# A hybrid encoder on one core: layer norm in a fixed order with five first columns, four gate tiles, a finish in PSUM

## The chip, the cores and the metric

The kernel runs on one core of a Trainium2 chip. A core has TensorE (PE) for matmuls, VectorE (DVE), ScalarE (ACT) and GpSimd (POOL) for elementwise work, and SyncE (SP), whose queue issues most DMA transfers. The metric is the device time of one execution in microseconds (us). Each number is compared as the median of several runs of one kernel on one chip.

## The reference

The reference is a small encoder of two layers over one sequence of 256 tokens and 2048 channels, in float32: a Conformer convolution module, a feed-forward block, a bidirectional gated DeltaNet, a feed-forward block, and a last RMSNorm. What matters here of it:

```python
def layernorm(x, g, b, eps=LN_EPS):
    xf = x.astype(jnp.float32)
    mu = jnp.mean(xf, axis=-1, keepdims=True)
    xc = xf - mu
    var = jnp.mean(xc * xc, axis=-1, keepdims=True)
    return (xc * lax.rsqrt(var + eps) * g.astype(jnp.float32) + b.astype(jnp.float32)).astype(x.dtype)

def conformer_conv_module(h, w_pw1, b_pw1, w_dw, b_dw, ln_g, ln_b, w_pw2, b_pw2):
    """pointwise D->2D + GLU -> depthwise conv (31, centred) -> LayerNorm over channels -> swish -> pointwise D->D."""
    u = h @ w_pw1 + b_pw1
    a, gate = jnp.split(u, 2, axis=-1)
    u = a * jax.nn.sigmoid(gate)
    u = depthwise_conv_centred(u, w_dw) + b_dw
    u = jax.nn.silu(layernorm(u, ln_g, ln_b))
    return u @ w_pw2 + b_pw2
...
```

The DeltaNet has 16 key heads and 32 value heads of 128 channels. Each value head gives an output o of 256 tokens by 128 channels; it is normed, multiplied with a gate silu(z) of its own, and the 32 gated heads together are multiplied with the output weights.

## The kernel before

All activations lie with channels on the 128 partitions and the 256 tokens along the free axis, so the 2048 channels are 16 tiles of 128 by 256. Float32 accuracy is kept by halves: a weight block of 128 by 512 (`CS` = 4 blocks of 128 inputs) is cast on ACT to `hi` (L172), and DVE takes the rest as `lo` = raw - hi (L173); activations are split the same way into a tile of 512 columns, high half and low half. A product of an input block with a column of 128 outputs is then a matmul of `hi` with 512 columns (L198) and one of `lo` with 256 (L197, L200): a pair. Elsewhere three matmuls of 256 columns do the same (L202 to L204).

Weights come in raw tiles of 8 input blocks (`CK`, 512 KB), issued on SP (L159), three of them in the pool (`RAW`), a further three of a second pool while `self.more` is set. `products` works several columns side by side (three first columns of a projection, which begin as soon as the first input tiles are there), `linear` one column. A scheduler places instructions by priority; a stretch under `manual_schedule` stands on DVE and ACT in the order in which it is written.

**End of the convolution module.** For each of 16 channel tiles j, 31 taps of the depthwise convolution are shared out: `NPE[j]` go to PE as matmuls with diagonal matrices (`r`, L373, two passes each), `NPOOL[j]` to ACT and POOL (ACT scales `m`, L381, POOL adds, L382), two to ACT and DVE alone, the rest to DVE (L388, L390). The results are added to the tile `a` (L394). The sum of a tile goes to PE (`s1`), its square `lsq` (ACT, L337) too (`s2`); after the last tile the mean `dm`, its square `dq` and the variance `var` follow on DVE, a square root on ACT, a reciprocal on DVE, and then for each tile a product, a difference, a silu, a cast and a difference for the low half `y` (L424 to L433). These are the inputs of the second pointwise projection (weights `pw2`), whose three first columns wait for `var` before their weights are split.

**DeltaNet.** `dn_gate` computes the gate of a head and stores it to `z_d`. `dn_heads` works a group of four value heads: outputs `ot` are scaled by `os`, transposed on PE (L945), copied by ACT (`on`, L947), multiplied with the gate on DVE (`zr`, L949 to L950) and stored to `y_d` (L951). There is one `zr` tile. A task with nothing left to wait for is taken up again step by step between the projections' columns; `gated` counts the gates done. Afterwards the out projection (weights `wout`) loads the 32 heads from `y_d` (four `y` tiles, L525), splits them into `ys` (L234, L235), and runs its three first columns.

**Finish.** After the last feed-forward block `finish` multiplies the 16 tiles with the reciprocal `rstd` (L986), every third on POOL, and issues 16 output transfers on SP and ACT in turn (L987).

## Time and profile before

| | |
|---|---|
| runs | 2828.8, 2833.96, 2838.57 us; median 2833.96 |
| the profiled execution | 2831.13 us, of it the span 2829.3 |
| mean granted clock of TensorE | 0.992 of full speed |
| PE busy | 2754.5 us, 97% |
| weight loads of PE | 2508.4 us, 89%, beside the matmuls |
| DVE busy | 2070.5 us, 73% |
| ACT busy | 1760.6 us, 62% |
| POOL busy | 367.6 us, 13% |
| DMA | 533.91 MB, mean 189 GB/s |

PE is the busy engine, and most of its time is in matmuls that follow one another without a pause. The chain of work that ended last is PE for 81% of the span, DVE for 6%, ACT and DMA for 5% each. The stages in time: first pointwise projection with the convolution until about 258 us, the norm and second projection until 362, the first feed-forward block, the DeltaNet's projections and heads from about 1100 to 1915, the out projection from about 1880, the second feed-forward block, and the finish from about 2815.

### The profile page before, as it was taken

What the parts mean: (1) busy time and instruction counts of PE and PEld (TensorE: products, weight loads), DVE (VectorE), ACT (ScalarE), POOL (GpSimd) and SP (SyncE); (2) the same over time, 40 slices, a digit from 0 to 9 for tenths busy, and PEclk for the clock granted to TensorE, in tenths of its full rate; (3) what the DMA queues carried; (4) which work ended last, traced back from release to release, by engine and by line L of the source; (5) the groups of instructions that cost most, each with busy time, mean ns of one, the idle gap of its engine ahead of it and who ended that gap; (6) DMA issues with size and microseconds to landing.
All of it is one profiled execution on the core that took longest, in us unless ns stands there. A gap on an engine that the chain in (4) does not pass through costs nothing.

```text
span 2829.3 us, 50192 instructions
## 1 busy us (share of the span) xinstructions
PE 2754.5 (97%) x18192; PEld 2508.4 (89%) x18192; DVE 2070.5 (73%) x3895; ACT 1760.6 (62%) x3710; POOL 367.6 (13%) x427
## 2 busy tenths in 40 slices
PE   8997999999999999999999999998999999999998
PEld 7997888888888889998999999987888888888887
DVE  8999876666666667898988989756666666665555
ACT  8877555555554445767878877764455555555443
POOL 3764310000000011000000000001110000000111
PEclk9998999999999999999999999999999999999999
DMA  5443665555666665765565655575566655566664
GB/s 186 142 142 97 194 210 191 187 191 188 190 190 191 197 201 176 246 219 189 185 218 187 201 194 195 178 237 184 189 209 190 189 190 190 188 190 186 189 190 138
DMA packets 171801, 533.91 MB, mean 189 GB/s; under 512 B 19073, under 2 KB 43905, under 8 KB 171553
## 3 DMA queue, kind: packets, MB, share of 16 engines
q1 hardware_dynamic: 170256, 529.42, 58.5%
q8 instruction: 142, 2.33, 0.3%
q10 hardware_dynamic: 1296, 1.30, 0.1%
q14 instruction: 107, 0.87, 0.1%
HBM read 501.22 MB, written 29.43 MB: 188 GB/s over the span
## 4 chain that ended last, share of the span: by engine, by line
PE 81%; DVE 6%; ACT 5%; DMA 5%; issue 2%; POOL 1%; SPq 0%; DVEq 0%; POOLq 0%; ACTq 0%
PE acc L198 40%; PE acc L197 20%; PE acc L204 5%; PE acc L203 5%; PE acc L202 5%; DVE lo L173 2%; POOL a L382 1%; DMA raw<-in_win 1%; ACT hi L172 1%; PE psa L852 1%; PE psb L894 1%; DMA y_d<-zr 1%; PE acc L200 1%; PE psb L917 1%; DVE r L390 1%
## 5 line engine op out<-in xcount | busy, mean ns | idle before, releaser
L173 DVE TENSOR_TENSOR lo<-raw,hi 128x512 fp32r<-128x512 f32 x1764 | 1259.7, 719 | 648.5 <-ACT hi L172 640.4
L172 ACT CAST hi<-raw 128x512 fp32r<-128x512 f32 x1764 | 1079.5, 619 | 839.9 <-PE acc L198 660.1
L198 PE MATMUL acc<-xs,hi 128*128 128x512 f32 x2816 | 967.3, 392 | 0.0
L197 PE MATMUL acc<-xs,lo 128*128 128x256 f32 x2640 | 743.5, 282 | 0.0
L198 PEld LDWEIGHTS acc<-xs,hi 128*128 128x128 f32 x2816 | 516.8, 188 | 100.0
L202 PE MATMUL acc<-xs,hi 128*128 128x256 f32 x2064 | 587.3, 286 | 15.5 <-ACT hi L172 9.2
L204 PE MATMUL acc<-xs,lo 128*128 128x256 f32 x2064 | 586.7, 285 | 3.8 <-DVE lo L173 3.8
L203 PE MATMUL acc<-xs,hi 128*128 128x256 f32 x2064 | 585.0, 284 | 0.9 <-DVE xs L251 0.7
L197 PEld LDWEIGHTS acc<-xs,lo 128*128 128x128 f32 x2640 | 498.2, 189 | 8.3
L198 PE MATMUL acc<-hs,hi 128*128 128x512 f32 x1408 | 486.8, 391 | 0.0
L202 PEld LDWEIGHTS acc<-xs,hi 128*128 128x128 f32 x2064 | 389.8, 189 | 21.7 <-ACT hi L172 12.3
L204 PEld LDWEIGHTS acc<-xs,lo 128*128 128x128 f32 x2064 | 389.5, 189 | 10.8 <-DVE lo L173 6.3
L203 PEld LDWEIGHTS acc<-xs,hi 128*128 128x128 f32 x2064 | 390.2, 189 | 7.5 <-issue 5.2
L197 PE MATMUL acc<-hs,lo 128*128 128x256 f32 x1376 | 388.1, 282 | 0.0
L198 PEld LDWEIGHTS acc<-hs,hi 128*128 128x128 f32 x1408 | 262.3, 188 | 53.4
L197 PEld LDWEIGHTS acc<-hs,lo 128*128 128x128 f32 x1376 | 259.9, 189 | 1.6
L198 PE MATMUL acc<-ys,hi 128*128 128x512 f32 x512 | 179.9, 396 | 8.6 <-DVE ys L235 8.6
L463 POOL TENSOR_TENSOR tg<-tg,rstd 128x256 f32<-128x256 f32 x88 | 65.5, 744 | 905.4 <-ACT tg L462 905.4
L382 POOL TENSOR_TENSOR a<-a,m 128x256 f32<-128x256 f32 x170 | 148.7, 875 | 97.5 <-ACT m L381 85.6
L197 PE MATMUL acc<-ys,lo 128*128 128x256 f32 x496 | 140.8, 286 | 2.6 <-DVE lo L173 2.5
L261 POOL TENSOR_TENSOR sq<-h 128x256 f32<-128x256 f32 x59 | 54.6, 925 | 548.7 <-DVE h L474 384.3
L638 DVE SCALAR_TENSOR_TENSOR u<-t,par_sb,u 128x254 f32<-128x254 f32 (+1 forms) x256 | 121.3, 482 | 1.4 <-ACT u L634 1.1
(229 smaller groups left out, 2910.0 us busy)
## 6 DMA issues: line engine op xcount, KB each, us to landing
raw<-in_gu SPq DMA_DIRECT2D x352, 512.0 KB, 4.4
raw<-in_win SPq DMA_DIRECT2D x194, 512.0 KB, 4.1
raw<-in_dn SPq DMA_DIRECT2D x160, 512.0 KB, 3.6
raw<-in_pw SPq DMA_DIRECT2D x94, 512.0 KB, 3.8
raw<-in_wout SPq DMA_DIRECT2D x64, 512.0 KB, 3.7
a_d<-am SPq DMA_DIRECT2D x32, 512.0 KB, 4.6
ar<-a_d SPq DMA_DIRECT2D x32, 512.0 KB, 4.8
raw<-in_dn SPq DMA_DIRECT2D x32, 256.0 KB, 3.6
```

The source lines that it names most:

```text
L172: nc.scalar.copy(hi, r)
L173: nc.vector.tensor_tensor(lo, r, hi.bitcast(F32), op=ALU.subtract)
L197: nc.tensor.matmul(acc[:, S:], lo, a[:, :S], start=False, stop=False)
L198: nc.tensor.matmul(acc, hi, a, start=first, stop=last)
L200: nc.tensor.matmul(acc[:, S:], lo, a[:, :S], start=False, stop=False)
L202: nc.tensor.matmul(acc[:, :S], hi, a[:, :S], start=first, stop=False)
L203: nc.tensor.matmul(acc[:, :S], hi, a[:, S:], start=False, stop=False)
L204: nc.tensor.matmul(acc[:, :S], lo, a[:, :S], start=False, stop=last)
L261: (nc.vector if last else nc.gpsimd).tensor_tensor(sq, h, h, op=ALU.mult)
L382: nc.gpsimd.tensor_tensor(acc, acc, m, op=ALU.add)
L463: nc.gpsimd.tensor_tensor(tg, tg, rstd, op=ALU.mult)
L638: nc.vector.scalar_tensor_tensor(u[:, lo:hi], t[:, lo + s : hi + s], w(i), u[:, lo:hi], op0=ALU.mult, op1=ALU.add)
```

## The change

1. The last channel tile of the convolution gives 12 taps to PE and 6 to POOL, 9 and 5 before; DVE gathers its partial sums in a tile `part` before it touches the tile. The table load for the square root moves behind the last tile's scalings.
2. Five raw tiles of `pw2` are issued, and their high halves cast on ACT, before the sums end. After the last sum PE gets 26 matmuls into a tile `idle` that nobody reads (`FILL`). From `dm` to the last low half the order on DVE and ACT is written by hand, `dq` goes to ACT, and the projection starts with five columns.
3. There are four `zr` tiles in a pool of their own. The four gates of a group are loaded ahead of its transposes. The last four heads' products stay in their tiles, and the out projection splits them from there.
4. In the finish the reciprocal is written to PSUM (`own`); DVE multiplies with it there, ACT makes a copy for POOL, which takes every fourth tile.
5. At the start `Square` of the first tile is written ahead of its scaling.

```diff
-NPE = [5] * 12 + [6, 6, 6, 9]
-NPOOL = [11] * 12 + [11, 11, 11, 5]
+NPE = [5] * 12 + [6, 6, 6, 12]
+NPOOL = [11] * 12 + [11, 11, 11, 6]
...
-XB = 6
+XB = 7
+FIRSTS = 5
+PRE = 5
+FILL = 26
...
                     if own:
-                        r.append(own)
-                    for o in r:
-                        nc.vector.tensor_tensor(acc, acc, o, op=ALU.add)
+                        self.more, self.five, self.more_raw = cv, 0, 2
+                        with tc.issue_after(self.raw_dma.ins):
+                            raws = [self.raw_weights(self.pw2[c], 0, CK) for c in range(FIRSTS)]
...
+                        with tc.issue_after(scaled.ins):
+                            self.warm(AF.Sqrt, tg)
+                            for c in range(PRE):
+                                pre_hi = highs(c)
+                    if own:
+
+                        part = new("part", 1)
+                        nc.vector.tensor_copy(part, own)
+                        for o in (r[1], r[0]):
+                            nc.vector.tensor_tensor(part, o, part, op=ALU.add)
+                        t = nc.vector.tensor_tensor(acc, acc, part, op=ALU.add)
+                        weights(0, t)
+                        weights(1, t)
...
-                if j == KD - 1:
-                    self.warm(AF.Sqrt, tg)
...
+            idle = self.ps.tile([P, 512], F32, tag="lin", bufs=PSB["lin"], name=self.nm("idle"))
+            with tc.issue_after(self.summed.ins):
+                for n in range(FILL):
+                    nc.tensor.matmul(idle, pre_hi[:, :P], pre_hi, start=True, stop=True)
...
+                nc.scalar.activation(dq, sums["s1"], AF.Square, scale=1.0 / D)
+                known = nc.vector.scalar_tensor_tensor(var, sums["s2"], 1.0 / D, dq, op0=ALU.mult, op1=ALU.subtract)
+                rt = self.sp.tile([P, S], F32, tag="rstd", bufs=2, name=self.nm("rstd"))
+                nc.scalar.activation(rt, var, AF.Sqrt, scale=1.0, bias=self.c("eps5"))
+                self.warm(AF.Silu, rt)
+                weights(2)
+                nc.vector.reciprocal(lr, rt)
                 nc.vector.tensor_tensor(ml, dm, lr, op=ALU.mult)
...
+                mul(0)
+                sub(0)
+                mul(1)
+                weights(3)
+                sub(1)
+                mul(2)
+                for n in range(KD):
+                    low(n)
...
-                first = self.products(self.pw2[:3], KD, ys, wide=True, tags=("lin", "lin", "g"), pool=cv, order=order)
+            with tc.issue_after(begun.ins):
+                self.ahead, self.split_ahead = [raws], pre[:PRE]
+                first = self.products(self.pw2[:FIRSTS], KD, ys, wide=True, tags=("lin", "lin", "lin", "g", "a")[:FIRSTS], pool=cv, order=order)
...
+                    if v < NVH - 4:
+                        y = o0.tile([P, S], F32, tag="y", bufs=4, name=self.nm("y"))
+                        nc.sync.dma_start(y, self.y_d[v])
+                    else:
+                        y = self.y_last[v % 4]
...
-        "cb": (2 * S, 2), "e": (768, 2), "am": (1024, 2), "ar": (1024, 2), "zr": (S, 1), "xd": (16 * P, 2),
+        "cb": (2 * S, 2), "e": (768, 2), "am": (1024, 2), "ar": (1024, 2), "zr": (S, 4), "xd": (16 * P, 2),
...
-        yield STEP + 1
+        zs = []
         for i in range(4):
             while self.gated <= 4 * g + i:
                 yield 1
+            zs.append(self.d("zr"))
+            nc.sync.dma_start(zs[i], self.z_d[4 * g + i])
+        yield STEP + 1
+        for i in range(4):
...
-            z = self.d("zr")
-            nc.sync.dma_start(z, self.z_d[4 * g + i])
+            z = zs[i]
             nc.vector.tensor_tensor(z, on, z, op=ALU.mult)
-            nc.sync.dma_start(self.y_d[4 * g + i], z)
+            if 4 * g + i < NVH - 4:
+                nc.sync.dma_start(self.y_d[4 * g + i], z)
...
-        rstd = self.pending()
+
+        own = self.ps.tile([P, S], F32, tag="b", bufs=PSB["b"], name=self.nm("own"))
...
+        nc.scalar.copy(rstd, own)
         for k in range(KD):
             o = self.h[k]
-            (nc.gpsimd if k % 3 == 1 else nc.vector).tensor_tensor(o, o, rstd, op=ALU.mult)
+            if k % 4 == 1:
+                nc.gpsimd.tensor_tensor(o, o, rstd, op=ALU.mult)
+            else:
+                nc.vector.tensor_tensor(o, o, own, op=ALU.mult)
```

On ACT, at the end of the convolution module, the kernel before has this from the sigmoid of the last tile on (`hi` are the weights' high halves, `rstd` the square root of the norm):

```order
L355 ACTIVATE tg_3558<-tg_3558,par_sb 128x256
L278 ACT_TABLE_LOAD
L278 ACTIVATE warm_3698<-tg_3558 128x1
L378 ACTIVATE a_743_3632<-up_231,par_sb,wdw 128x256
...
L381 ACTIVATE m_3677<-up_231,wdw 128x256
L337 ACTIVATE lsq_3701<-a_743_3632 128x256
L172 CAST hi_3827<-raw_3821 128x512
...
L172 CAST hi_3871<-raw_3825 128x512
L283 ACTIVATE rstd_3712<-var_3708,cst_sb 128x256
```

And the changed kernel, in the same place:

```order
L369 ACTIVATE tg_3558<-tg_3558,par_sb 128x256
L392 ACTIVATE a_743_3632<-up_231,par_sb,wdw 128x256
...
L395 ACTIVATE m_3689<-up_231,wdw 128x256
L292 ACT_TABLE_LOAD
L292 ACTIVATE warm_3713<-tg_3558 128x1
L414 CAST hi_3715<-raw_3703 128x512
...
L181 CAST hi_3934<-raw_3705 128x512
L351 ACTIVATE lsq_3738<-a_743_3632 128x256
L466 ACTIVATE dq_3769<-s_274_1316 128x256
L469 ACTIVATE rstd_3794<-var_3770,cst_sb 128x256
```

The table load has moved behind the scalings `m` (five before, six now), and seven casts `hi` stand ahead of `lsq` where six stood behind it.

On SP, in the body of the DeltaNet, the gates of heads 8 to 11 are loaded and their products stored in the kernel before as follows (rows between left out; `zr<-z_d` is the load, `y_d<-zr` the store, `raw` weights):

```order
L951 DMA y_d7_12618<-zr_3712_17945 128x256
L949 DMA zr_3954_19195<-z_d8_12587 128x256
...
L951 DMA y_d8_12619<-zr_3954_19195 128x256
L949 DMA zr_3961_19224<-z_d9_12588 128x256
L159 DMA raw_4235_20480<-in_win 128x1024
...
L951 DMA y_d9_12620<-zr_3961_19224 128x256
L159 DMA raw_4246_20529<-in_win 128x1024
L949 DMA zr_3974_19269<-z_d10_12589 128x256
```

And in the changed kernel:

```order
L1017 DMA zr_3937_19126<-z_d8_12624 128x256
L1017 DMA zr_3938_19128<-z_d9_12625 128x256
L168 DMA raw_3927_19051<-in_win 128x1024
L1028 DMA y_d6_12654<-zr_3657_17680 128x256
L1028 DMA y_d7_12655<-zr_3658_17682 128x256
L1017 DMA zr_3939_19130<-z_d10_12626 128x256
...
L1028 DMA y_d8_12656<-zr_3937_19126 128x256
L1028 DMA y_d9_12657<-zr_3938_19128 128x256
L1017 DMA zr_4154_20068<-z_d12_12628 128x256
```

A load that stood right behind the store of the head before it now stands in pairs behind the stores of the group before, and the stores of a group come in pairs.

On DVE, in the tail of the DeltaNet, the kernel before has this from the product of head 29 on (`zr` the product, `ys` the split of a head, `lo` the weights'):

```order
L950 TENSOR_TENSOR zr_4940_23860<-on_4939_23858,zr_4940_23860 128x256
L173 TENSOR_TENSOR lo_5085_24338<-raw_5079_24327,hi_5084_24337 128x512
L173 TENSOR_TENSOR lo_5087_24366<-raw_5077_24323,hi_5086_24365 128x512
L950 TENSOR_TENSOR zr_4943_23869<-on_4942_23867,zr_4943_23869 128x256
L950 TENSOR_TENSOR zr_4946_23878<-on_4945_23876,zr_4946_23878 128x256
L235 TENSOR_TENSOR ys_5017_24057<-y_5016_24055,ys_5017_24057 128x256
```

And the changed kernel, from the product of head 30 on:

```order
L1026 TENSOR_TENSOR zr_4943_23890<-on_4950_23909,zr_4943_23890 128x256
L182 TENSOR_TENSOR lo_5085_24362<-raw_5080_24353,hi_5084_24361 128x512
L1026 TENSOR_TENSOR zr_4944_23892<-on_4952_23915,zr_4944_23892 128x256
L182 TENSOR_TENSOR lo_5087_24366<-raw_5081_24355,hi_5086_24365 128x512
L182 TENSOR_TENSOR lo_5089_24394<-raw_5079_24351,hi_5088_24393 128x512
L244 TENSOR_TENSOR ys_5023_24093<-y_5022_24091,ys_5023_24093 128x256
L244 TENSOR_TENSOR ys_5025_24098<-y_5024_24096,ys_5025_24098 128x256
L244 TENSOR_TENSOR ys_5026_24101<-zr_4941_23886,ys_5026_24101 128x256
```

The splits of heads 28 to 31 now read the tiles `zr` themselves; before, every split from head 26 on stood behind the product of head 31.

## Rows read from the trace of the kernel before

**Rows 1.** The page, busy time: engine, busy us, share of the span, instructions.

```profile
PE 2754.5 (97%) x18192; PEld 2508.4 (89%) x18192; DVE 2070.5 (73%) x3895; ACT 1760.6 (62%) x3710; POOL 367.6 (13%) x427
```

**Rows 2.** Windows: stretch, us, busy us by engine, granted clock, DMA share, GB/s.

```profile
250.00:275.00 25.00, 11.41 (x43) 9.04 (x44) 23.12 (x58) 16.08 (x35) 3.62 (x5) 0.66 0.19 64
1175.00:1878.00 703.00, 681.67 (x5716) 658.63 (x5716) 609.10 (x1337) 539.48 (x1355) 26.42 (x14) 1.00 0.61 202
...
1900.00:1926.40 26.40, 15.67 (x91) 12.98 (x89) 9.00 (x18) 11.13 (x26) 1.91 (x1) 0.85 0.48 158
1926.40:1932.40 6.00, 6.00 (x18) 5.03 (x19) 3.56 (x8) 2.37 (x5) 0.00 (x0) 0.50 0.24 71
```

**Rows 3.** Timeline of PE, 244 to 296: start, us, instruction, count, [idle before, releaser].

```profile
250.11 4.15 PE L373 MATMUL r<-up,diag 128*128 128x256 f32 x18 [0.25 <-DVE up L356]
258.03 1.22 PE L327 MATMUL s<-a,cst_sb 128*128 128x256 f32 x2 [3.77 <-DVE a L394]
...
269.82 0.80 PE L198 MATMUL acc<-y,hi 128*128 128x512 f32 x1 [9.72 <-DVE y L433]
...
273.68 0.51 PE L197 MATMUL acc<-y,lo 128*128 128x256 f32 x3
...
277.86 0.52 PE L197 MATMUL acc<-y,lo 128*128 128x256 f32 x3
```

**Rows 4.** Timeline of ACT in the same stretch.

```profile
249.55 1.28 ACT L278 ACT_TABLE_LOAD   x1
...
251.45 2.09 ACT L381 ACTIVATE m<-up,wdw 128x256 f32<-128x256 f32 x5
...
258.33 3.21 ACT L172 CAST hi<-raw 128x512 fp32r<-128x512 f32 x6
```

**Rows 5.** Timeline of DVE in the same stretch.

```profile
250.49 0.48 DVE L388 TENSOR_SCALAR own<-up,wdw 128x256 f32<-128x256 f32 x1
...
255.19 0.48 DVE L390 SCALAR_TENSOR_TENSOR own<-up,wdw,own 128x256 f32<-128x256 f32 x1
...
260.63 3.69 DVE L173 TENSOR_TENSOR lo<-raw,hi 128x512 fp32r<-128x512 f32 x6
264.24 1.76 DVE L287 RECIPROCAL ln<-rstd 128x256 f32<-128x256 f32 x1
...
266.37 0.75 DVE L424 TENSOR_TENSOR a<-a,ln 128x256 f32<-128x256 f32 x2
```

**Rows 6.** Timeline of POOL in the same stretch.

```profile
252.02 3.93 POOL L382 TENSOR_TENSOR a<-a,m 128x256 f32<-128x256 f32 x5 [4.27 <-ACT m L381]
```

**Rows 7.** Waits of SP's queue, 1090 to 1935: us in total, times, longest.

```profile
SPq L949 <- DMA y_d<-zr: 58.2, 31, 3.9
```

**Rows 8.** Waits of DVE, 1178 to 1878, same columns.

```profile
DVE zr L950 <- DMA zr<-z_d: 18.6, 10, 5.0
```

**Rows 9.** Chain of work that ended last, tail of DeltaNet: start, us, what.

```profile
1908.15 5.05 DMA y_d<-zr
...
1917.96 3.20 DMA zr<-z_d
```

**Rows 10.** Timeline of PE in the tail of DeltaNet.

```profile
1917.22 0.51 PE L197 MATMUL acc<-ys,lo 128*128 128x256 f32 x3
1926.36 1.65 PE L198 MATMUL acc<-ys,hi 128*128 128x512 f32 x3 [8.63 <-DVE ys L235]
```

**Rows 11.** Timeline of ACT in the same stretch.

```profile
1914.53 1.14 ACT L172 CAST hi<-raw 128x512 fp32r<-128x512 f32 x2 [0.97 <-DMA raw<-in_wout]
```

**Rows 12.** The page, DMA issues: count, KB each, median us to landing.

```profile
raw<-in_wout SPq DMA_DIRECT2D x64, 512.0 KB, 3.7
```

**Rows 13.** Timeline of the finish, DVE and POOL.

```profile
2819.61 6.42 DVE L986 TENSOR_TENSOR h<-h,rstd 128x256 f32<-128x256 f32 x11
2819.65 4.41 POOL L986 TENSOR_TENSOR h<-h,rstd 128x256 f32<-128x256 f32 x5 [17.49 <-DVE rstd L287]
```

**Rows 14.** Windows in the finish, columns as in rows 2.

```profile
2826.00:2828.00 2.00, 0.00 (x0) 0.00 (x0) 0.02 (x1) 0.00 (x0) 0.00 (x0) 0.50 1.09 378
```

166 lines of the change are left out of this document (96 added, 70 removed).

## Prediction

> **What bounds the kernel now.** I read the busy table first: PE works 2754.5 us of 2829.3 [rows 1], so the kernel is a string of matmuls with some 75 us of holes, and what a change can win is a hole, or a stretch at low clock. Second the windows, to find the holes: the end of the convolution module has PE busy 11.41 of 25 us at a mean granted clock of 0.66; the tail of DeltaNet, from 1900 to 1926.4, 15.67 of 26.4, and the 6 us behind it run at 0.50, which is 1.2 of 2.4 GHz; the body of DeltaNet loses 21 us spread thinly over 703 [rows 2]. Third the timelines of these places and the chain of waits, which name what each hole waits for [rows 3 to 12]. The finish behind the last matmul counts in full [rows 13, 14]. Feed-forward and the middles of the projections have no hole; the change touches them little.
>
> **The sum's base.** The profiled execution took 2831.13 us, 1.8 more than its span; the median of the runs is 2833.96. I take the gains off both and forecast on the median.
>
> **Part 1, end of the convolution module.** PE finishes its taps at 254.26, waits 3.77 us for the last tile, and after the two sums waits 9.72 us until the first y matmul at 269.82 [rows 3]. It then works cold: six pairs (a 512- and a 256-column matmul) from 269.82 to 273.68, 0.64 each, then twelve up to 277.86, 0.35 each [rows 3].
> The last tile: DVE's taps come every 0.39 us (twelve from 250.49 to 255.19) [rows 5]; four fewer save 1.56, an added copy costs 0.3. PE's 24 passes instead of 18 at 0.23 (4.15/18) [rows 3] end at 255.6, and POOL's six adds at 0.79 (3.93/5) [rows 6] at 255.9, since the table load of 1.28 that stood ahead of the last tile's scalings [rows 4] moves behind them. Both are hidden behind DVE, so the tile is ready near 256.7 instead of 258.0.
> ACT: tile, six scalings of 0.42 (2.09/5), load, then seven casts of 0.54 (3.21/6) end at 258.3 [rows 4]. The new order puts those casts ahead of the square lsq, which begins at 258.3 instead of beside the sum at 258.03 [rows 3]: what the tile won is lost again here, and s2, var and the sums behind it wait for that. In return sqrt no longer stands behind six casts, and DVE has one lo split instead of six (3.69) between var and the reciprocal. lsq 0.4, s2 0.6, var 0.4 and sqrt 0.5 put the reciprocal at 260.8 instead of 264.24 [rows 5]. Before, 5.58 us passed from there to the first y matmul; now tile 0 goes to ACT after one product and one difference, and I count 5.0, so y is ready at 265.8.
> Fillers: 26 matmuls of 512 columns stand on PE between s2 (done near 259.5) and the first y matmul, which cannot pass them. A 512-column matmul is two thirds of a pair: 0.23 warm, 0.43 cold. All warm they end at 265.6 and cost nothing, as the norm hides them. The windows show a low clock after a hole lasting 3.9 us here and 6.0 at 1926.4 [rows 2, 3]; with as much of it the fillers end between 267.4 and 268.4 and delay PE. Either way y starts warm, which saves 6 x 0.29 = 1.75.
> The Trainium skill (TensorE: Matmul & The Clock Gate, Part 1: The HAM clock gate) calls the half clock the default state, released by activity; by it the fillers pay the cold stretch themselves. The gain would be 1.4 + 1.75 = 3.2 with it, 4.0 + 1.75 = 5.8 without; the trace agrees that a hole of 9.72 us is followed by cold matmuls [rows 3] and cannot show which holds after two holes of 1.5 us.
> Five first columns instead of three: 80 pairs at 0.35 are 28 us, in which DVE has 16 x 3 norm steps at 0.33 and 16 splits at 0.6, 26 us, so PE stays the bound by a little. The second raw tiles must land beside it; I allow 0 to 1.2 us of stall. Then 11 columns remain instead of 13, the same matmuls in all. **Gain 4, between 1 and 5.8.**
>
> **Part 2, body of DeltaNet.** One zr tile makes each head's z load wait on SP until the store of the head before has landed, 58.2 us in 31 waits, and DVE stands 18.6 us in the body for z [rows 7, 8]. With four tiles and the loads ahead of the transposes, these loads wait once per pair of heads. But behind SP's wait stand weight loads that run ahead of their use, and PE's whole loss is 21 us, most of it for other reasons (chains of small products between ACT and DVE). On the other side the four loads now hold back a group's transposes until all four gates exist, and the third and fourth loads queue on SP ahead of weights. A new order of everything costs or wins some us: **gain 2, between -5 and 8.**
>
> **Part 3, tail of DeltaNet.** The last four heads go round zr by zr: product, store (5.05 for head 28), load, product, store, load (3.20 for head 30), and so on [rows 9]. PE's last matmul before the hole is at 1917.22, then it waits 8.63 us to 1926.36 for the ys splits, which stand on DVE behind zr of head 31 [rows 10]. Eighteen pairs (six heads by three columns) are left: 6.0 us cold hold 9.4 pairs, 8.6 more at 0.35 need 3.0, so they end at 1935.4.
> After: the last transposes stand in the same place of PE's queue, behind the third column of heads 20 to 23, near 1914.5; ACT's copy and DVE's product give zr of head 31 by 1916.1. Then come two splits of weights (0.6 each) and six ys splits of 0.33, to 1919.4; no store and no load is among them. The weights of these columns had landed by 1914.53 [rows 11]. PE waits at most 0.5 us, works warm, and needs 18 x 0.35 = 6.3 us from 1917.5: it ends near 1924. That is 11.4 earlier. Behind it the next column's weights must come: their buffer is free at about 1917 and a landing takes 3.7 us in the median [rows 12], so 1920.7; a cast of 0.54 and a split of 0.6 leave some 2 us. **Gain 11, between 6 and 12.**
>
> **Part 4, finish and start.** Eleven DVE products take 6.42 us, 0.58 each, beside five of POOL at 0.88 [rows 13]. After the change DVE's second operand lies in PSUM. The rows for that kind are 0.33 to 0.38 (two in 0.75, POOL idle) and 0.39 (taps on own and r, POOL adding) [rows 5, 6]. Twelve at 0.39 end at 2824.3 instead of 2826.03; POOL's copy of 0.4 and four at 0.88 end earlier, at 2823.6. The output is 2 MB, though, and the last window already moves 378 GB/s [rows 14]; begun at 2820, it cannot end before 2825.5. **Gain 1.3, between -0.6 (if DVE stays at 0.58 for twelve) and 2.** The Trainium skill (SBUF — State Buffer, SBUF: two separate sides) says that a DVE instruction with two SBUF inputs and a GpSimd one exclude each other for a whole instruction; one with a single SBUF input would be free of that. By it the gain is 1.7 less what DMA keeps; without it, -0.6. The taps, unslowed at 0.39 while POOL adds, speak for it.
> At the start Square of h0 stays ahead of xs0 as it stood: nothing.
>
> **Sum.** 4 + 2 + 11 + 1.3 = 18.3. The profiled execution becomes 2812.8, the median 2815.7; I say 2815.5. A measurement here tells 0.3%, 8.5 us, from no change.
>
> **Rivals.**
> Tail fed by weights: three raw tiles, freed only as DVE splits, land late, and PE waits for them instead of for ys. For: the last of them had landed only at 1914.53, with ACT waiting 0.97 [rows 11]. Against: SP issued them between stalled zr transfers, now gone. The gain is 4 instead of 11: 2822.5. Chance 0.12.
> Body wins more: if z's waits on DVE are what holds back the matmul feeders, half of PE's 21 us goes: 2807.5. Chance 0.12.
> Fillers do not do their work: all cold they end at 259.5 + 26 x 0.43 = 270.7, later than y's 269.82 of before; a late start by 0.9 against 1.75 saved leaves 0.9, and a stall of 1 leaves nothing: 2819.7. Chance 0.10.
> Slower: in the body PE executes in order, and a transpose that stands at its head until four z tiles exist and are gated stops all matmuls behind it. Priced at the longest wait of SP for zr, 3.9 us [rows 7], once per group of eight it costs 31 us: 2815.5 + 2 + 31 = 2848. It decides from about 2.5 us per group, where no gain is left. Against: transposes stand where they stood, and DVE's split work has slack. Chance 0.04. A milder form of it (1.5 to 3 us a group), or the bad ends of tail and body together, ends within 0.3%: 0.10.
>
> **How the numbers follow.** Forecast 0.52, between 2809 and 2822; rivals 0.12, 0.12, 0.10, 0.04, and 0.10 for a result near no change. All but the last two are faster by over 0.3%, with a few hundredths of them falling short of it: faster 0.84, same 0.12, slower 0.04. The range takes in the tail's and the filler rival together (about 2827) and the body's better end (2804): 2804 to 2828.
>
> **What would show it.** In the convolution window 250 to 275 PE busy with fillers and the first y matmul before 268.5, without the 0.64 pairs. Between 1900 and 1930 no PE wait for ys over 1 us and a granted clock of 1.00. SP's wait of zr for y_d below 30 us, PE busy in the body no less than 681 of 703. DVE's last products at 0.39 each. Wrong, if a PE wait for raw weights follows the tail, if y starts after 269, or if the body's span grows.

## The result and the profile after

The changed kernel takes 2806.19 us in the median of four runs (2802.27 to 2809.28), the kernel before 2832.56 on the same chip: a ratio of 0.9897, 95% interval 0.9882 to 0.9912. It gains 26.4 us, where 18.3 were forecast. The time lies in the range of 2804 to 2828, but 9.3 us below the predicted 2815.5. The profiled execution took 2802.27, its span 2800.5 against 2829.3.

The busy line answers to [rows 1]: PE does the same work, and what went is idle time and time at low clock.

```profile
PE 2754.0 (98%) x18224; PEld 2510.1 (90%) x18224; DVE 2065.2 (74%) x3892; ACT 1759.7 (63%) x3716; POOL 367.9 (13%) x427
```

The windows answer to [rows 2], in its columns. In the end of the convolution module PE is busy 21.91 of 25 us (11.41 before; 6.27 of the 21.91 are the 26 matmuls that nobody reads) at a clock of 1.00 (0.66); in the tail of DeltaNet, 1900 to 1926.4, 26.33 of 26.4 (15.67) at 1.00 (0.85).

```profile
250.00:275.00 25.00, 21.91 (x104) 17.56 (x105) 22.88 (x55) 19.18 (x39) 4.37 (x6) 1.00 0.17 53
1160.00:1862.00 702.00, 690.33 (x5819) 669.40 (x5818) 617.78 (x1356) 547.64 (x1378) 28.11 (x14) 1.00 0.63 208
...
1900.00:1926.40 26.40, 26.33 (x151) 23.17 (x152) 21.08 (x39) 14.78 (x29) 5.48 (x7) 1.00 0.62 199
```

Three starts cut the program at nearly the same work in these two kernels (10598 matmuls between the first two before, 10594 after): the first low-half matmul of the first feed-forward block (first `acc<-xs,lo`), the first of the out projection (first `acc<-ys,lo`) and the last of its sixteen columns. These are the groups of one line of PE with count, ns (shortest, median, longest) and first and last start, of before:

```profile
L200 PE MATMUL acc<-xs,lo x176: 281/282/469, 362.5 to 2564.8; 128*128 128x256 f32 x176
...
L200 PE MATMUL acc<-ys,lo x16: 281/282/283, 1878.8 to 2068.7; 128*128 128x256 f32 x16
```

and of after:

```profile
L209 PE MATMUL acc<-xs,lo x176: 281/281/468, 360.0 to 2537.1; 128*128 128x256 f32 x176
...
L209 PE MATMUL acc<-ys,lo x16: 280/281/282, 1862.9 to 2040.9; 128*128 128x256 f32 x16
```

From the first to the third mark, called **the stretch** below, before takes 2068.7 - 362.5 = 1706.2 us, after 1680.9. Its first piece (feed-forward and body of DeltaNet) falls from 1516.3 to 1502.9, its second (tail and out projection) from 189.9 to 178.0.

| part | forecast | measured in the two profiles |
|---|---|---|
| 1, convolution end (last matmul of the first projection to the first mark) | 4 | 114.85 to 110.9: 3.95 |
| 2, body | 2 (-5 to 8) | 13.4 |
| 3, tail | 11 (6 to 12) | 11.9 |
| 4, finish (last matmul to the end) | 1.3 | 14.62 to 13.51: 1.1 |

These sum to 30.4; the first projection itself ended 1.4 later in this execution, which leaves the 28.8 of the spans. Parts 1, 3 and 4 are near their forecasts in this profile. Part 2 is the miss, and the experiments are about it. This execution is the fastest of its four, though. A second profile of the same kernel (2807.50 us, the row "again" in the table of the experiments) gives 2.8 for part 1, 10.8 for the body, 9.4 for the tail and 1.1 for the finish.

**The end of the convolution.** Timeline of PE, columns as in [rows 3]:

```profile
251.55 5.45 PE L387 MATMUL r<-up,diag 128*128 128x256 f32 x24 [0.25 <-DVE up L370]
258.36 0.70 PE L341 MATMUL s<-a,cst_sb 128*128 128x256 f32 x2 [1.36 <-DVE a L435]
260.20 0.70 PE L341 MATMUL s<-lsq,cst_sb 128*128 128x256 f32 x2 [1.14 <-ACT lsq L351]
260.54 6.27 PE L456 MATMUL idle<-hi 128*128 128x512 f32 x26
267.00 0.50 PE L207 MATMUL acc<-y,hi 128*128 128x512 f32 x1 [0.19 <-DVE y L484]
```

The holes of 3.77 and 9.72 have become 1.36, 1.14 and 0.19, and the first y pair runs warm. The second profile has the same two holes (1.36 and 1.15), but its fillers run partly at a granted clock of 0.50, and the first y matmul, at 267.56, starts only as they end:

```profile
260.19 7.53 PE L456 MATMUL idle<-hi 128*128 128x512 f32 x26
```

ACT and DVE in the first profile, in the same stretch:

```profile
258.69 1.13 ACT L181 CAST hi<-raw 128x512 fp32r<-128x512 f32 x2
259.73 0.41 ACT L351 ACTIVATE lsq<-a 128x256 f32<-128x256 f32 x1
...
261.47 0.51 ACT L469 ACTIVATE rstd<-var,cst_sb 128x256 f32<-128x256 f32 x1 [1.06 <-DVE var L467]
```

```profile
257.88 0.42 DVE L435 TENSOR_TENSOR a<-a,part 128x256 f32<-128x256 f32 x1
...
262.01 1.76 DVE L472 RECIPROCAL ln<-rstd 128x256 f32<-128x256 f32 x1
```

Less the 1.44 us by which all this began later, the tile is ready at 256.9 (256.7 worked out), `lsq` starts at 258.3 (258.3), the reciprocal at 260.6 (260.8), y at 265.6 (265.8). Behind that the saving stops: from the first y matmul to the first mark it takes 92.97 us, 92.66 before, although y begins warm. PE waits 1.51 us there, 0.28 before.

**The tail.** Where PE waited 8.63 us [rows 10], the longest wait from 1900 to the last mark is 0.85 us, and it is for weights. DVE splits the last four heads out of the tiles `zr`, with no store and no load among them. In the second profile PE waits 3.42 us for weights earlier on: the raw tile for them took 7.31 us to land, 5.79 in the first profile. Timelines of PE and DVE, and of PE in the second profile:

```profile
1900.07 0.39 PE L206 MATMUL acc<-ys,lo 128*128 128x256 f32 x1 [0.85 <-DVE lo L182]
```

```profile
1900.54 0.75 DVE L244 TENSOR_TENSOR ys<-y,ys 128x256 fp32r<-128x256 f32 x2
1901.21 1.42 DVE L244 TENSOR_TENSOR ys<-zr,ys 128x256 fp32r<-128x256 f32 x4
```

```profile
1881.52 0.58 PE L206 MATMUL acc<-ys,lo 128*128 128x256 f32 x1 [3.42 <-DVE lo L182]
```

**The finish**, against [rows 13]: DVE 0.34 for each product (0.58 before), POOL 0.69 (0.88).

```profile
2792.32 4.07 DVE L1073 TENSOR_TENSOR h<-h,own 128x256 f32<-128x256 f32 x12 [0.44 <-ACT rstd L1067]
2792.37 2.77 POOL L1071 TENSOR_TENSOR h<-h,rstd 128x256 f32<-128x256 f32 x4 [17.90 <-ACT rstd L1067]
```

**SP's waits for the gates did not shrink.** Against the 58.2 us of [rows 7] stand 24.4 for the stores of `zr` and, new, 36.0 for the stores of the gates themselves, since the loads now stand early enough to meet them: 60.4 in all. DVE's wait for a gate in the body [rows 8] is gone. Waits of SP's queue (us in total, times, longest):

```profile
SPq L1017 <- DMA z_d<-s: 36.0, 14, 4.7
...
SPq L1017 <- DMA y_d<-zr: 24.4, 12, 3.5
```

### The profile page after: what moved, and what is told of

It is laid out like the page before. It is cut to its first block, busy times and chain, and to the rows that moved or that the text cites. A ratio compares the mean times of both kernels' runs of the same rounds, so it can differ in the third digit from the quotient of the medians.

```text
span 2800.5 us, 50212 instructions
## 1 busy us (share of the span) xinstructions
PE 2754.0 (98%) x18224; PEld 2510.1 (90%) x18224; DVE 2065.2 (74%) x3892; ACT 1759.7 (63%) x3716; POOL 367.9 (13%) x427
## 4 chain that ended last, share of the span: by engine, by line
PE 82%; ACT 6%; DVE 4%; DMA 4%; issue 2%; POOL 2%; SPq 0%; POOLq 0%; DVEq 0%; ACTq 0%
PE acc L207 39%; PE acc L206 20%; PE acc L213 5%; PE acc L212 5%; PE acc L211 5%; POOL a L396 2%; DVE lo L182 2%; PE psa L925 1%; PE psb L967 1%; ACT hi L181 1%; DMA raw<-in_win 1%; PE psb L990 1%; PE acc L209 1%; DMA raw<-in_wout 1%; PE psg L778 1%
## 5 line engine op out<-in xcount | busy, mean ns | idle before, releaser
L211 PE MATMUL acc<-xs,hi 128*128 128x256 f32 x2064 | 585.7, 285 | 13.7 <-ACT hi L181 8.9
L213 PEld LDWEIGHTS acc<-xs,lo 128*128 128x128 f32 x2064 | 389.6, 189 | 11.9 <-issue 5.7
```

What stands on the lines that cost most here:

```text
L211: nc.tensor.matmul(acc[:, :S], hi, a[:, :S], start=first, stop=False)
L213: nc.tensor.matmul(acc[:, :S], lo, a[:, :S], start=False, stop=last)
```

## Experiments

Two explanations of the body's 13.4 us stand against each other. By the first, the gate code itself (its four tiles, its early loads, the heads kept on chip) is worth more than I priced. By the second, the order: the scheduler, which places every instruction of the DeltaNet by priority, lays the whole of it out in another way as soon as anything ahead of it changes, and this layout happened to be a good one. The expectations number their theories as they stood when each was written, and call the scheduler the planner; the text between them calls the theories by what they say. Medians and ratios are against the kernel before on the same chip; "stretch" is from the profiled execution.

| kernel | median us | ratio, 95% interval | stretch |
|---|---|---|---|
| before (first profile) | 2832.56 | 1 | 1706.2 |
| the change | 2806.19 | 0.9897, 0.9882 to 0.9912 | 1680.9 |
| the change, again, five runs | 2803.33 | 0.9900, 0.9886 to 0.9914 | 1686.0 |
| gates_only | 2822.91 | 0.9967, 0.9955 to 0.9979 | 1697.0 |
| gates_stored | 2824.50 | 0.9973, 0.9963 to 0.9982 | 1707.8 |
| tiles4 | 2828.33 | 0.9983, 0.9973 to 0.9992 | 1700.5 |
| conv_finish | 2827.97 | 0.9979, 0.9965 to 0.9992 | 1702.3 |
| before_npe12 | 2835.07 | 0.9998, 0.9988 to 1.0007 | 1708.7 |
| after_11_7 | 2822.11 | 0.9962, 0.9948 to 0.9976 | 1697.1 |
| after_13_6 | 2807.04 | 0.9899, 0.9884 to 0.9913 | 1685.0 |
| after_9_5 | 2814.27 | 0.9926, 0.9911 to 0.9941 | 1692.1 |
| no_fill | 2808.72 | 0.9913, 0.9897 to 0.9928 | 1690.0 |
| first3 | 2819.33 | 0.9950, 0.9935 to 0.9965 | 1691.4 |
| lsq_first | 2803.49 | 0.9895, 0.9880 to 0.9911 | 1682.7 |
| after_stored | 2810.25 | 0.9917, 0.9899 to 0.9935 | 1689.8 |
| a117_zpool | 2810.54 | 0.9917, 0.9900 to 0.9933 | 1692.7 |
| after_zpool | 2802.64 | 0.9894, 0.9879 to 0.9909 | 1680.7 |
| lsq_zpool | 2800.81 | 0.9887, 0.9869 to 0.9904 | 1682.9 |

### The parts one by one

`gates_only` is the kernel before with the DeltaNet code of the change; `gates_stored` is that with the last four heads going round by `y_d` again; `tiles4` changes one number of the kernel before; `conv_finish` is the change with the DeltaNet code of before.

```
# gates_stored, against gates_only
-                    if v < NVH - 4:
-                        y = o0.tile([P, S], F32, tag="y", bufs=4, name=self.nm("y"))
-                        nc.sync.dma_start(y, self.y_d[v])
-                    else:
-                        y = self.y_last[v % 4]
+                    y = o0.tile([P, S], F32, tag="y", bufs=4, name=self.nm("y"))
+                    nc.sync.dma_start(y, self.y_d[v])
...
-            if 4 * g + i < NVH - 4:
-                nc.sync.dma_start(self.y_d[4 * g + i], z)
+            nc.sync.dma_start(self.y_d[4 * g + i], z)
# tiles4, against before
-"zr": (S, 1)
+"zr": (S, 4)
```

> The kernel before with the gate part of the change alone: four zr tiles, loads ahead of the transposes, last four heads kept on chip; convolution module and finish as before. In the changed kernel the stretch from the first matmul of the first feed-forward block to the first matmul of the out projection was 13.4 us shorter and the tail 11.9. Theory 1 (both come from this part alone, whatever stands ahead): 25 us faster than before, ratio 0.991, SP's wait of zr for y_d near zero, DVE's wait for z gone. Rival (a part of the body's gain comes with the other phase that the shorter convolution module gives the DMA queues): the body gives 2 to 8 as I predicted, in all 13 to 20 us, ratio 0.993 to 0.9955.

> The gate part alone, but the last four heads are stored to y_d and loaded again as before. Against gates_only it prices the keeping of four heads on chip. Body as in gates_only (11 to 13 us shorter than before). Tail: four stores and four loads side by side, 2 to 3.5 us each way, so PE waits 4 to 6 us for the splits of head 28 and works cold behind it if the hole is long: 5 to 8 us slower than gates_only, ratio to before 0.993 to 0.9945. If the order of DVE alone had made the tail's hole (splits behind the products), then the hole is under 2 us and the ratio within 0.001 of gates_only.

> The kernel before with one number changed: four zr tiles instead of one. Each load stands where it stood, behind its head's transposes, and all heads still go through y_d. Theory 1 (the body's gain is the wait of SP's queue for the store of the head before, 58.2 us in 31, gone with the tiles): the body is 10 to 13 us shorter than before, and in the tail the round trips overlap, 5 to 9 more: 15 to 22 us faster, ratio 0.992 to 0.995. Theory 2 (the gain comes with the new places of loads, transposes and all that the scheduler moved with them): body within 3 us of before, tail 5 to 9: ratio 0.996 to 0.998.

> The changed kernel with the DeltaNet as before (one zr tile, round trips): convolution module, finish and start are those of the change. Theory 1 (the parts add up): 4 us from the convolution module and 1.1 from the finish, 5 us faster than before, ratio 0.998, body and tail of DeltaNet as before within 2 us. Rival (a shift of phase by the shorter convolution module changes the body too): body moves by 3 us or more against before.

The gate part alone shortens the stretch by 9.2 us, far from the 25.3 of the change, and less than the 13 that I had forecast for it. The four tiles alone give 5.7. With the DeltaNet code untouched, `conv_finish` still shortens it by 3.9. By medians the gate part brings 9.2 us and the rest 4.1, 13.3 together, and the change brings 26.4: the parts do not add up. That speaks against the gate code as the whole cause. It does not yet speak for the order: the 4.1 of `conv_finish` are about what parts 1 and 4 are worth (5 together), and the 3.9 in its stretch come from a profile near its fastest run (2823.03, median 2827.97). `tiles4`, 0.9983, is nearer to the weaker of its two expectations and decides nothing by itself: it has an order of its own. The profile of `gates_stored` is its slowest run (2833.91); by medians the store costs 1.6 us there, not the 5 to 8 expected. What came is the alternative that its expectation names last: a ratio within 0.001 of `gates_only`, and no hole of PE over 2 us in the tail. Its longest wait for the out projection:

```profile
1918.15 0.39 PE L197 MATMUL acc<-ys,lo 128*128 128x256 f32 x1 [1.74 <-DVE lo L173]
```

`tiles4`, which still sends every head through `y_d`, has no hole over 2.6 us in the tail either. `conv_finish`, with one tile, has two of 6.51 and 6.90. So the hole of 8.63 us [rows 10] goes with the one tile, whether the last heads stay on the chip or not.

These kernels also test the rival "body wins more", whose time, 2807.5, is nearest to the result, and whose mechanism was DVE's wait for z. In the first piece of the stretch PE was not busy for 21.3 us before and 11.7 after; in `gates_only`, where DVE has no such wait left, for 16.5; in `conv_finish`, where DVE still waits 13.7 us for z, for 13.4. So the gain does not follow DVE's wait for z. Nor has one large wait gone; the largest became somewhat shorter. Waits of PE in that piece, before and after:

```profile
PE pssum L668 <- ACT sq L656: 3.9, 3, 2.4
PE acc L202 <- DVE t L633: 3.0, 2, 1.6
```

```profile
PE pssum L741 <- ACT sq L729: 2.4, 4, 1.1
PE acc L211 <- DVE t L706: 2.1, 2, 1.8
```

### The order alone

Three kernels move one or a few taps of the last channel tile between the engines, some 100 us ahead of the stretch, and change nothing else of the change; a fourth does it to the kernel before. The instructions of the DeltaNet are the same in the first three. `after_13_6` keeps the order of the change there; `after_11_7` and `after_9_5` get two others, and that of `after_11_7` is nearly that of `gates_only`.

```
# after_11_7 (after_13_6: 13 and 6, after_9_5: 9 and 5)
-NPE = [5] * 12 + [6, 6, 6, 12]
-NPOOL = [11] * 12 + [11, 11, 11, 6]
+NPE = [5] * 12 + [6, 6, 6, 11]
+NPOOL = [11] * 12 + [11, 11, 11, 7]
# before_npe12, against before
-NPE = [5] * 12 + [6, 6, 6, 9]
-NPOOL = [11] * 12 + [11, 11, 11, 5]
+NPE = [5] * 12 + [6, 6, 6, 12]
+NPOOL = [11] * 12 + [11, 11, 11, 6]
```

> The changed kernel with one tap of the last convolution tile moved from PE to POOL (11 and 7 instead of 12 and 6). The convolution module should lose 0.3 to 0.8 us (one more add of 0.79 on POOL). But the planner then lays out the whole DeltaNet in another order: of DVE's 3895 instructions some 800 stand elsewhere, with the same gate code. Theory 3 (the body's extra gain was the order that the planner happened to find): from the first feed-forward matmul to the last column of the out projection 1688 to 1698 us instead of 1680.9, ratio to before 0.993 to 0.996. Rival (the extra gain comes from the gates and the shorter convolution module acting together, whatever the order): within 1.5 us of the changed kernel, ratio 0.989 to 0.9905.

> The changed kernel with one more tap of the last convolution tile on PE (13 instead of 12), one less on DVE. Here the planner's order in the DeltaNet is that of the changed kernel, row for row. Theory 3 (order): the same as the changed kernel within 1 us, stretch 1680 to 1682 us, ratio to before 0.989 to 0.990. Rival (the time of the DeltaNet hangs on small shifts of phase at its beginning, not on the order): the stretch moves by 3 us or more although the order is the same.

> The changed kernel with the old shares of the last convolution tile (9 taps on PE, 5 on POOL, 15 on DVE). The convolution module should lose 1.0 to 1.6 us (four taps of 0.39 on DVE). The planner's order in the DeltaNet is a third one. Theory 3 (order): the stretch from the first feed-forward matmul to the last column of the out projection differs from 1680.9 by 4 us or more, 1685 to 1698, ratio to before 0.992 to 0.996. Rival (gates and convolution module act together): only the 1 to 1.6 us are lost, ratio 0.9895 to 0.991.

> The kernel before with the new shares of the last convolution tile alone (12 taps on PE, 6 on POOL). The convolution module gains 0.5 to 1.5 us at its end. The DeltaNet's code is untouched, but about a fourth of DVE's instructions there stand elsewhere in the planner's order. Theory 3 (order): the stretch from the first feed-forward matmul to the last column of the out projection differs from the 1706.2 of before by 3 us or more, either way. Rival (without the gate part the order does not matter, since the waits for the stores set the pace): within 2 us of 1706.2, ratio 0.9990 to 1.0000.

The order makes the difference. One tap moved costs up to 16 us: `after_11_7` has a stretch of 1697.1, that of `gates_only` within 0.1, and `after_13_6`, with the change's order row for row, 1685.0, inside the scatter of that order (1680.9 to 1690.0 in five profiles of four kernels). By medians on one chip `after_11_7` and `after_13_6` lie 15.1 us apart, 1.7 of them ahead of the stretch in their profiles. `after_9_5`, with a third order, lies between, at 1692.1, as expected. (For `after_13_6` 1680 to 1682 was expected, and a move of 3 us or more was the mark of its rival, small shifts of phase. It moved 4.1; but the change itself moved 5.1 from its first profile to its second, so that much is scatter.) `before_npe12` misses its expectation: it has another order too, its stretch is 2.5 us longer, its total the same. Not every new order matters.

The second mark of the stretch does not cut every kernel at the same work: in `gates_only` and `after_11_7` the out projection begins 40 matmuls earlier than before. Windows of PE from the first mark to the 10600th matmul behind it (stretch, us, PE busy, granted clock, DMA share, GB/s) compare the body fairly; in order, before, the change, the change again, `gates_only`, `after_11_7`:

```profile
362.48:1878.83 1516.35, 1495.02 (x10600) 1.00 0.61 198
359.97:1863.53 1503.56, 1491.89 (x10600) 1.00 0.63 200
360.42:1866.50 1506.08, 1494.16 (x10600) 1.00 0.60 200
362.11:1876.37 1514.26, 1497.21 (x10600) 1.00 0.59 198
362.25:1876.64 1514.39, 1496.86 (x10600) 1.00 0.62 198
```

Cut so, the gate code shortens the body by 2.1 and 2.0 us in the order of `gates_only` and `after_11_7`, and by 12.8 and 10.3 in the order of the change. The rest of the stretch takes 189.9 us before, 177.3 and 180.0 in the change, 182.7 and 182.6 in the two others.

Where the 16 us between these two profiles are can be read. `after_11_7` has two holes of PE that the change has not (timeline of PE):

```profile
1516.83 3.68 PE L925 MATMUL psa<-w,z 128*128 128x64 f32 x16 [5.08 <-ACT z L933]
```

```profile
1888.55 0.58 PE L206 MATMUL acc<-ys,lo 128*128 128x256 f32 x1 [4.44 <-DVE lo L182]
```

and `gates_only` has the first of them in the same place:

```profile
1516.48 3.67 PE L856 MATMUL psa<-w,z 128*128 128x64 f32 x16 [5.09 <-ACT z L864]
```

The windows of `after_11_7`, columns as in [rows 2], show that the granted clock behind each hole is 0.50, 1.2 of 2.4 GHz:

```profile
1511.75:1516.83 5.08, 0.00 (x1) 0.01 (x1) 0.00 (x0) 4.91 (x15) 0.00 (x0) 0.82 0.00 0
1516.83:1525.00 8.17, 8.17 (x38) 8.17 (x39) 6.92 (x15) 7.07 (x16) 0.00 (x0) 0.50 0.38 128
...
1888.55:1893.90 5.35, 5.35 (x20) 4.81 (x20) 2.08 (x5) 3.80 (x15) 0.00 (x0) 0.50 0.93 308
```

5.08 + 8.17/2 + 4.44 + 5.35/2 is about 16 us, all of the difference between 1697.1 and 1680.9. (The second hole is not the order's alone: the change's second profile has one of 3.42 us near that place.) The chain of waits that leads to the first hole (start, us, what):

```profile
1494.31 3.83 DMA y_d<-zr
...
1498.20 0.32 SPq L1017
...
1499.05 5.60 DMA raw<-in_win
...
1504.74 0.62 ACT hi L181
1505.36 0.52 ACT pb L906
...
1516.41 0.37 ACT z L933
1516.83 3.68 PE psa L925 x16
```

A gate's load stands on SP (L1017) until a head's store has landed; a weight load behind it starts late and lands at 1504.65; ACT waits with its cast; only then come some 10 us of copies (`pb`, `bl`, `stk`, L906 and L821) and the `z` for which PE waits. So part of what makes this order dear may be the queue of SP, where weights stand behind a load that waits.

### Gate loads on another queue

To test that, the gates are loaded on POOL's queue, in the bad order (`a117_zpool`) and in the good one (`after_zpool`). The edit moves the order a little itself: of DVE's 2467 instructions in the stretch 25 stand elsewhere in `a117_zpool` than in `after_11_7`, and 182 in `after_zpool` than in the change.

```
-            nc.sync.dma_start(zs[i], self.z_d[4 * g + i])
+            nc.gpsimd.dma_start(zs[i], self.z_d[4 * g + i])
```

> The run with 11 and 7 taps, but the gate loads (zr) are issued on POOL's queue instead of SP's; the order on DVE stays that of the run with 11 and 7 taps but for 40 rows. Theory 4 (a hole comes where a weight load stands on SP behind a gate load that waits for a store): the hole of 5.08 us at about 1512 and the 8 us at half clock behind it are gone, the hole of 4.44 us at about 1884, behind a load of y, stays: 7 to 10 us faster than the run with 11 and 7 taps, ratio to before 0.9925 to 0.994. Rival (the order on ACT makes the hole, its 10 us of copies ahead of z, not SP): the hole stays over 3 us, ratio 0.9955 to 0.997.

> The changed kernel with the gate loads (zr) issued on POOL's queue instead of SP's. In the changed kernel SP still waits 60 us for stores ahead of these loads, but no hole of PE over 2 us follows. Theory 4 (such waits cost only where a weight load comes too late for PE): no gain, within 2 us of the changed kernel, ratio to before 0.989 to 0.9905. Rival (SP's waits cost everywhere a little): 4 us or more faster, ratio under 0.9885.

In the bad order it gives back some 12 of the 16 us (2822.11 to 2810.54 on two chips; as ratios 0.9962 to 0.9917), somewhat more than expected; by the intervals it lies between 7 and 19 us. The profiled execution, its slowest with 2815.66, shows 4.4 of them in the stretch. Timeline of PE in `a117_zpool`:

```profile
1512.24 3.42 PE L925 MATMUL psa<-w,z 128*128 128x64 f32 x16 [2.52 <-ACT z L933]
```

```profile
1882.08 0.39 PE L206 MATMUL acc<-ys,lo 128*128 128x256 f32 x1 [0.87 <-DVE lo L182]
...
1892.07 0.36 PE L206 MATMUL acc<-ys,lo 128*128 128x256 f32 x1 [1.18 <-DVE lo L182]
```

The first hole is halved, not gone; that ACT's copies, which still stand ahead of `z`, make the rest of it is not shown. The second, which I expected to stay, shrank to 0.87 and 1.18. In the good order, or one near it, the queue makes no difference that can be told, as expected: 2802.64. So SP's wait is part of what a bad order costs; it is not what the change gained.

### The tail: kept on chip, or stored

`after_stored` is the change with the last four heads going by `y_d`, the same edit as in `gates_stored`, in the order of the change.

> The changed kernel, but the last four heads are stored to y_d and loaded again; the planner's order up to the last splits is that of the changed kernel. Theory (keeping them on chip removes the hole of the tail): the four stores and loads go side by side, the splits of head 28 come 5 to 8 us later than 1901.2, PE has a hole of 4 to 7 us and 2 to 3 us of low clock behind it: 6 to 9 us slower than the changed kernel, ratio to before 0.9915 to 0.993. Rival (four tiles alone remove it, since the round trips overlap): hole under 2 us, ratio 0.9895 to 0.9905.

The time rises by 4 us against the change's first median and 7 against its second, on other chips (the ratio by 0.0017 to 0.0020, some 5 us, intervals overlapping), where 6 to 9 were expected, and the tail takes 185.9 us against 178.0 and, in the change's second profile, 180.5. The single hole of 4 to 7 us did not appear: the loss is spread over several waits. Timeline of PE:

```profile
1880.09 0.58 PE L206 MATMUL acc<-ys,lo 128*128 128x256 f32 x1 [3.56 <-DVE lo L182]
...
1910.02 0.62 PE L206 MATMUL acc<-ys,lo 128*128 128x256 f32 x3 [1.24 <-ACT ys L243]
```

The change's second profile too has a wait of over 3 us near 1880, so that one is scatter. In this order, then, some 5 of the tail's 9 to 12 us come from keeping the heads on chip (185.9 against 180.5), in the order of `gates_only` 1.6 by medians; the rest comes already with four tiles and the order around them.

### The end of the convolution

`no_fill` leaves out the 26 matmuls that nobody reads. `first3` works three first columns. `lsq_first` moves the two casts ahead of `lsq` behind the square root.

```
# no_fill
-FILL = 26
+FILL = 0
# first3
-FIRSTS = 5
-PRE = 5
+FIRSTS = 3
+PRE = 3
...
-                weights(3)
# lsq_first
-                nc.scalar.activation(rt, var, AF.Sqrt, scale=1.0, bias=self.c("eps5"))
+                dqi = nc.scalar.activation(rt, var, AF.Sqrt, scale=1.0, bias=self.c("eps5"))
...
-            with tc.issue_after(begun.ins):
+            with tc.issue_after(begun.ins), tc.issue_after(dqi.ins):
```

> The changed kernel without the 26 filler matmuls; the order in the DeltaNet is that of the changed kernel. Theory (the fillers are hidden by the norm and keep the clock up): PE stands idle for some 6 us from s2 to the first y matmul, starts at the same place, and runs its first pairs at 0.64 instead of 0.35 for 3 to 6 us, as behind the hole of 9.72 us before: 1.4 to 2.7 us lost, ratio to before 0.990 to 0.991, granted clock of 250 to 275 below 0.9. Rival (PE's own taps end so late that the clock does not fall): clock 1.00, nothing lost, y 0.2 us earlier.

> The changed kernel with three first columns and three splits ahead, as before, instead of five. The DeltaNet's order becomes that of the run with 9 and 5 taps, so only the convolution module is read: from the first y matmul to the first of the next block the changed kernel takes 92.6 us. Theory (three columns are too little work for PE while DVE makes y: 48 pairs of 0.35 are 16.8 us, DVE needs 48 norm steps of 0.33 and 9 splits of 0.6, 21 us): 2 to 4 us more, 94.5 to 96.5. Rival (PE lives on DVE's lead, as before the change): 91.5 to 93 us. The whole: ratio to before 0.992 to 0.995.

> The changed kernel with two of the seven weight casts moved on ACT from ahead of the last square lsq to behind the square root; the DeltaNet's order unchanged. In the changed kernel lsq began at 259.73 although its tile was ready at 258.30. Theory (these casts hold the norm): lsq begins 1.0 us earlier, and s2, var, the reciprocal and the first y matmul too: from the last matmul of the first projection to the first y matmul 16.9 us instead of 17.9, about 1 us faster than the changed kernel, ratio to before 0.989 to 0.9898. Rival (the fillers end no earlier, or the two casts now hold the first silu): within 0.3 us of 17.9.

Without fillers PE has a hole of 6.10 us and begins y cold; from the last matmul of the first projection to the next block it takes 113.2 us instead of 110.9, 2.3 more, within what was expected. Against the change's second profile, with its fillers partly cold (112.1), it is 1.1 more. Timeline and window of `no_fill`:

```profile
265.48 0.80 PE L207 MATMUL acc<-y,hi 128*128 128x512 f32 x1 [6.10 <-DVE y L484]
```

```profile
250.00:275.00 25.00, 16.40 (x66) 12.99 (x66) 22.83 (x55) 19.39 (x40) 4.37 (x6) 0.73 0.14 42
```

With three columns the stage from the first y matmul to the next block takes 99.6 us instead of 92.6, more than the 2 to 4 that I expected: PE catches up with the norm, waits for y and loses the clock. (Its DeltaNet has nearly the order of `after_9_5`, so its total mixes two causes.) Timeline of `first3`:

```profile
260.58 8.87 PE L456 MATMUL idle<-hi 128*128 128x512 f32 x26
...
277.07 0.63 PE L206 MATMUL acc<-y,lo 128*128 128x256 f32 x3 [2.38 <-ACT y L481]
...
279.95 1.01 PE L206 MATMUL acc<-y,lo 128*128 128x256 f32 x3 [1.00 <-ACT y L481]
```

The same row shows the fillers partly cold: 8.87 us, 6.27 in the change, behind the same two waits of 1.4 and 1.1 us. So do those of most kernels here: of six profiles with these two waits only the change's first and `conv_finish` ran them in under 7 us. In `lsq_first` the square starts a microsecond earlier, and the way from the last matmul of the first projection to the first y matmul falls from 17.93 to 17.23 us; 1.0 was expected. The second of the two waits is gone there, and both kernels with this edit (`lsq_first`, `lsq_zpool`) ran the fillers in 6.29 us; in the change's second profile the way took 19.2. The total cannot be told from the change.

### The best of them, beside the change

> The changed kernel as it is, on the chip of the next run, to measure its scatter. 2803 to 2809 us, ratio to before 0.9885 to 0.9905; the stretch from the first feed-forward matmul to the last column of the out projection 1679 to 1686 us.

> The changed kernel with two weight casts behind the square root and the gate loads on POOL's queue. If the gains add (0.7 us seen in the convolution module of lsq_first, 0 to 3 in the DeltaNet of after_zpool): 1 to 4 us faster than the changed kernel on the same chip, ratio to before 0.9875 to 0.9892. If the DeltaNet's part was scatter: 0.5 to 1 us faster, not told apart.

`lsq_first` with the gate loads on POOL's queue takes 2800.81 (2800.10 to 2802.46) beside 2803.33 (2803.15 to 2807.50) for the change on the same chip. It is the lowest median of all, but the intervals of the two ratios overlap, so it is not shown to be faster than the change.

## Why the prediction was right and wrong

**Failed: part 2, the body, 2 between -5 and 8, measured 13.4 and, in the second profile, 10.8.** The step that failed is the term with which it ends: "a new order of everything costs or wins some us". It stands in the sum at next to nothing, and no row is named for its bounds. The gate's own part was priced about right, as far as one order shows it: in the order that `gates_only` and `after_11_7` share, the same gate code shortens the body by 2.1 and 2.0 us. What the sum left out is the order: that of the change makes it 12.8 and 10.3, 8 to 11 us more, and in the whole stretch the two orders lie some 13 us apart by medians on one chip (`after_13_6` and `after_11_7`). Three orders of one gate code shorten the stretch by 9.1, 14.1 and 16 to 25 us, on both sides of the 13 that parts 2 and 3 sum to, so that the change got a good order was luck. The bounds had to be drawn from what a layout can do: before, PE lost 21 us in the body at small waits [rows 2], of which the change's first profile has 9.7 fewer; the other 3.7 of its 13.4 lie in time that the profile counts as busy, and what they are is not shown. Why the scheduler finds this order with 12 taps and the other with 11 stays open, and I know of no row of before from which it could have been read.

**Right in time, not in mechanism: the rival "body wins more".** Its 2807.5 is nearest to the result, by luck. Its condition, that z's waits on DVE hold back the matmul feeders, fell with `gates_only`, where these waits are gone and the body gains 2.1 us.

**Right in size, in part by luck: part 1.** 3.95 against 4, and 2.8 in the second profile. Up to the first y matmul each step is within 0.3 us of what was worked out. The fillers were warm in the first profile (6.27 us) and cost nothing; for that branch the working gives 5.8, and 1.85 of it did not come: the 1.75 for warm pairs does not show in the time behind y, 92.97 us against 92.66, of which 1.2 are new waits of PE, the top of the stall that was allowed. In the second profile they were partly cold (7.53 us) and held y back, and 2.8 stands against the 3.2 of that branch. The Trainium skill (TensorE: Matmul & The Clock Gate, Part 1: The HAM clock gate) makes half speed the default, so that the fillers would pay the cold stretch. The change's first trace (6.27) shows none, its second (7.53) and that of `first3` (8.87) show a part of one, so a run can go either way after these waits. Five first columns, which I priced at a stall of 0 to 1.2, are what keeps PE fed: with three the stage takes 7 us more.

**Right in size, not in mechanism: part 3.** 11.9 against 11, and 9.4 in the second profile. The working credits the end of the stores and loads; `gates_stored` and `tiles4` keep them and lose the hole of 8.63 us all the same, and keeping the heads on chip is worth some 5 us in the change's order and 1.6 in the other. Nor is the term a property of the edit alone: in the order of `gates_only` and `after_11_7` the same code shortens this piece by 7.1 and 7.3 us. The rival of weights that land late did not come in the first profile, whose longest wait from 1900 on is 0.85 us; it came in part in the second (3.42) and in `after_11_7` (4.44).

**Right: part 4.** 1.1 against 1.3. DVE's products take 0.34, not the 0.39 I took, and POOL beside it sped up as well, from 0.88 to 0.69. That agrees with the Trainium skill (SBUF — State Buffer, SBUF: two separate sides): a DVE instruction with one operand in PSUM does not shut GpSimd out.

**Signs.** PE from 250 to 275, PE's busy time in the body (690 of 702), the tail from 1900 without long waits: as announced in the first profile. DVE's last products took 0.34, not 0.39. SP's wait of `zr` for `y_d` below 30 us: true by the letter, 24.4, but not in what was meant. The loads now meet the stores of the gates, 36.0 more, and the 60.4 in all are no less than before; a load that moves ahead of one store meets another. The rival "slower", transposes that stop PE until four gates exist, did not come: no wait of PE in the body names a gate.

## What to carry to other kernels

Where a scheduler places instructions by priority, an edit is two edits: what it does, and the new order of everything behind it. Price the second from the holes that a layout could open or close (here some 13 us, as much as any part of the edit was worth), and before crediting an edit with a gain or blaming it for a loss, time the same code in two or three orders that a neutral nudge upstream gives. A load that waits for a store should not share a queue with weights that run ahead: in a bad order that cost some 12 us by medians, in a good one nothing that could be told, and one cannot choose the order.

## What the runs showed of the hardware

A short hole of PE can cost nearly twice its length: 5.08 us idle were followed by 8.17 us at a granted clock of 0.50 (1.2 of 2.4 GHz), 4.44 us by 5.35. The same code behind the same two waits of 1.4 and 1.1 us ran its 26 fillers in 6.27 and 7.53 us in two profiles of the change, and in 6.29, 7.34, 7.59 and 8.87 us in four other kernels, so whether so short a pause loses the clock differs from run to run. One instruction order of the stretch took 1680.9 to 1690.0 us in five profiles of four kernels, 1680.9 and 1686.0 in two of the change itself, so a difference of less than 9 us between two single profiles says little.
